# Layer 0 of a two-layer encoder: narrow weight chunks out, 512-column moving operands in, convolution run over two blocks at a time

## The chip, the cores and the metric

The kernel runs on one core of one Trainium2 chip. The metric is the device time of one execution in microseconds (us); the time before is the median of three runs. The engines are named as in the profile: PE (TensorE, the matrix unit), DVE (VectorE), ACT (ScalarE), POOL (GpSimd) and SP (SyncE, which issues the DMA transfers).

## What is computed

Two residual layers work on x, 256 positions by 2048 channels, all in fp32. Layer 0 is the one that the change touches; layer 1 (a gated linear recurrence in both directions) has the same outer form. Cut to layer 0, the reference is:

```python
h = rms_norm(x, conv_norm)                       # 256 x 2048
u = h @ w_in                                     # 2048 x 6144
a, b, z = jnp.split(u, 3, axis=-1)
v = a * jax.nn.sigmoid(b)
v = depthwise_conv(v, dw, taps=31, centred) + dw_b
v = jax.nn.silu(layer_norm(v, ln_g, ln_b))       # over the 2048 channels
x = x + (v * jax.nn.silu(z)) @ w_out             # 2048 x 2048
```

The layer norm runs over all channels at one position, so nothing behind it can start before the convolution of the last channel is there.

## The kernel before

**Products in high and low parts.** TensorE takes its operands in a rounded format (fp32r). So every fp32 weight piece (1 MB, `raw`, three buffers, loaded by SP) is cast by ACT to a high part `wh` (L133) and the remainder `wl` = raw - wh is taken (L134), by POOL for the in-projection of layer 0 (pieces 1 to 47; pieces 0 and 2 on DVE) and by DVE from piece 48 on. There are three buffers of each, so the cast of a piece waits until PE has done with the piece three before, and the load of a piece waits until the subtraction three before is done. The activations stand likewise as `hx`, high part and low part side by side. A product is wh·hi + wh·lo + wl·hi.

**The in-projection of layer 0.** The 2048 channels are taken in eight chunks j of 256. For each come a product `pa` (a) and a product `pb` (b), two weight pieces each (8 k-blocks of 128 input channels by 256 columns); after all eight, the eight products `pz` (the gate z). For j >= 2 a product is one `ws_chunk` (L207, which runs `ws_half`, L157 to L159, twice): 96 matmuls of 256 columns, all into one PSUM bank that holds both halves of the chunk. For j = 0 and 1 the work goes in half chunks of 128 channels (`ws_narrow`, L203 to L205). Layer 1 has another form, `pair_chunk` (L171 and L178): its moving operand is 512 columns, the high part and the low part of `hx` together, so a piece takes 16 matmuls of 512 columns with wh and 16 of 256 with wl. The result then has its wh·lo part in the other half of the bank, a chunk takes two banks, and a copy (ACT, L823) and an addition (DVE, L824) fold it. PSUM has four banks for all these products (tag "mm"), used in turn; a product begins when the bank that it takes has been read by its last reader.

**The convolution.** When pb of a chunk is done, ACT takes the sigmoid and DVE multiplies (`glu`). Then the 31 taps: ACT makes the first (`conv_start`, L411) and four more as products that POOL adds up (L423, L425); DVE makes the other 26 as fused multiply-adds with the accumulator in PSUM (L436) and the final sum `y` (L445). The two 128-channel blocks of a chunk are taken in turn, tap by tap, from j = 2 on; those of j = 0 and 1 each alone, behind their narrow chunk. POOL adds the finished blocks into a sum for the mean (L454, L456).

**Layer norm and gate.** After the last block PE forms the mean (`mu_ps`, L464), DVE subtracts it (L478), ACT squares, PE forms the variance (`var_ps`, L490), and then DVE goes chunk by chunk through scaling (L501), gain and offset (L508), products with the gate (L513, L514) and the low part (L516). Among these stand the gates of z: a sigmoid on ACT (L567) and a product on DVE (L570), which is the last reader of the bank of that `pz`. The out-projection of layer 0 (`po`, L195 to L197) needs all of it; behind it comes layer 1, whose first product is `psq`.

**What sets the order.** Each engine works through its own instructions in the order in which the program writes them. The program writes the matmuls piece by piece and, between them, work of the other engines, as given by a small estimate of their times: `later(LAG, glu)` puts a step off by LAG us of estimated time, the convolution is a generator that is charged TAP us for each tap, and the weight casts of piece i + 2 are written as piece i is begun. The constants are in a few lines at the top; what they set is only where in an engine's order a step stands.

## Time and profile before

| | us |
|---|---|
| median of three runs | 1007.8 |
| the three runs | 1007.01, 1007.8, 1008.5 |
| the profiled execution | 1008.56 |
| its span, first to last instruction | 1006.5 |
| PE busy in the span | 984.4 (98%) |
| DVE busy | 763.6 (76%) |
| ACT busy | 529.3 (53%) |
| POOL busy, all of it before 301 us | 254.0 (25%) |

The profiled execution took 1008.56 us in all, 2.1 us more than its span, and lies 0.76 us above the median. Layer 0 fills the first 401.8 us: the normalization and the first transposes to about 14 us, the a and b products to 212 us, the z products to 307.7 us, the out-projection to 401.8 us. What follows is layer 1, which the change leaves as it is.

### The profile page before, as it was taken

Reading aid. Unit: us, or ns where it says so; the run is one execution under the profiler, and the core shown is the slowest. Engines: PE = TensorE matmul, PEld = TensorE weight load, DVE = VectorE, ACT = ScalarE, POOL = GpSimd, SP = SyncE. Lnnn points to the kernel's source line nnn. Section 1 sums busy time; section 2 is a strip of 40 time slices with the busy share of each in tenths; the row PEclk is TensorE's granted clock in tenths of the full one; section 3 lists DMA queues with packets and bytes.
Section 4 is the critical chain, followed back from the end, with each engine's and each line's share of the span. In section 5 each row is a group of like instructions: output and inputs, shape, how many; then the busy total and the mean of one; then the engine's idle time right before and its main releaser. Section 6 shows DMA issues by size and latency. Waiting matters only on the chain.

```text
span 1006.5 us, 16189 instructions
## 1 busy us (share of the span) xinstructions
PE 984.4 (98%) x6657; PEld 876.4 (87%) x6657; DVE 763.6 (76%) x1228; ACT 529.3 (53%) x601; POOL 254.0 (25%) x107
## 2 busy tenths in 40 slices
PE   4999999999999999999999999999999999999998
PEld 4999999999997888888888888888888888888886
DVE  4587989888699455676878968889688897888552
ACT  6664655553656444555464644647456465465431
POOL 2499999999760000000000000000000000000000
PEclk9999999999999999999999999999999999999999
DMA  7765655555636655656545455554554536445561
GB/s 221 185 199 168 192 184 174 186 187 170 206 129 207 194 183 172 204 168 194 174 140 188 142 170 168 165 169 143 192 167 161 174 127 210 133 161 168 173 204 42
DMA packets 143995, 173.45 MB, mean 172 GB/s; under 512 B 2946, under 2 KB 109715, under 8 KB 143763
## 3 DMA queue, kind: packets, MB, share of 16 engines
q1 hardware_dynamic: 143922, 172.42, 53.1%
q8 instruction: 52, 0.85, 0.4%
q14 instruction: 21, 0.17, 0.1%
HBM read 170.31 MB, written 2.10 MB: 171 GB/s over the span
## 4 chain that ended last, share of the span: by engine, by line
PE 85%; POOL 5%; DVE 4%; DMA 3%; issue 2%; ACT 1%; SPq 0%; POOLq 0%; DVEq 0%; ACTq 0%
PE psaf L171 6%; PE psq L171 6%; PE psab L171 6%; PE lv L699 3%; POOL wl L134 3%; PE psaf L178 3%; PE psq L178 3%; PE psab L178 3%; PE po L196 3%; PE psz L195 3%; PE po L197 3%; PE pq L195 3%; PE po L195 3%; PE pq L196 3%; PE psz L197 3%; PE psv L195 3%
## 5 line engine op out<-in xcount | busy, mean ns | idle before, releaser
L133 ACT CAST wh<-raw 128x2048 fp32r<-128x2048 f32 (+1 forms) x172 | 306.6, 1788 | 296.8 <-issue 42.3
L134 DVE TENSOR_TENSOR wl<-raw,wh 128x2048 fp32r<-128x2048 f32 (+1 forms) x120 | 261.6, 2183 | 133.5 <-ACT wh L133 129.5
L134 POOL TENSOR_TENSOR wl<-raw,wh 128x2048 fp32r<-128x2048 f32 (+1 forms) x52 | 213.1, 4117 | 45.2 <-ACT wh L133 45.0
L436 DVE SCALAR_TENSOR_TENSOR acc<-vb,dw,acc 128x256 f32<-128x256 f32 x416 | 168.1, 482 | 7.5 <-ACT acc L411 6.4
L676 ACT COPY x<-T 128x512 f32<-128x512 f32 x88 | 55.9, 670 | 52.3 <-DVE T L684 51.9
L159 PE MATMUL pz<-hx,wl 128*128 128x256 f32 x256 | 72.6, 284 | 0.9 <-POOL wl L134 0.9
L157 PE MATMUL pz<-hx,wh 128*128 128x256 f32 x256 | 73.0, 285 | 0.0
L158 PE MATMUL pz<-hx,wh 128*128 128x256 f32 x256 | 72.4, 283 | 0.0
L171 PE MATMUL psaf<-hx,wh 128*128 128x512 f32 x256 | 63.5, 395 | 0.0
L171 PE MATMUL psab<-hx,wh 128*128 128x512 f32 x256 | 63.3, 394 | 0.0
L684 DVE TENSOR_TENSOR T<-T,pb 128x512 f32<-128x512 f32 x96 | 61.8, 685 | 1.3 <-PE lv L699 1.0
L171 PE MATMUL psq<-hx,wh 128*128 128x512 f32 x256 | 62.3, 392 | 0.0
L171 PEld LDWEIGHTS psq<-hx,wh 128*128 128x128 f32 x256 | 47.2, 188 | 9.6 <-DVE hx L247 0.3
L159 PE MATMUL pa<-hx,wl 128*128 128x256 f32 x192 | 54.7, 285 | 0.7 <-POOL wl L134 0.7
L159 PE MATMUL pb<-hx,wl 128*128 128x256 f32 x192 | 54.4, 284 | 0.2 <-POOL wl L134 0.2
L171 PEld LDWEIGHTS psaf<-hx,wh 128*128 128x128 f32 x256 | 46.4, 188 | 9.4
L158 PE MATMUL pb<-hx,wh 128*128 128x256 f32 x192 | 54.3, 283 | 0.0
L158 PE MATMUL pa<-hx,wh 128*128 128x256 f32 x192 | 54.3, 283 | 0.0
L157 PE MATMUL pb<-hx,wh 128*128 128x256 f32 x192 | 54.3, 283 | 0.0
L157 PE MATMUL pa<-hx,wh 128*128 128x256 f32 x192 | 54.3, 283 | 0.0
L171 PEld LDWEIGHTS psab<-hx,wh 128*128 128x128 f32 x256 | 46.4, 188 | 9.0
L707 DVE COPY_PREDICATED sd<-mask,lv 64x256 f32<-64x256 uint8 (+1 forms) x104 | 48.9, 470 | 7.0 <-PE lv L699 4.3
(201 smaller groups left out, 2320.1 us busy)
## 6 DMA issues: line engine op xcount, KB each, us to landing
raw<-in_hgrn_w_in SPq DMA_DIRECT2D x80, 1024.0 KB, 5.2
raw<-in_conv_w_in SPq DMA_DIRECT2D x47, 1024.0 KB, 5.3
raw<-in_conv_w_out SPq DMA_DIRECT2D x16, 1024.0 KB, 5.1
raw<-in_hgrn_w_out SPq DMA_DIRECT2D x16, 1024.0 KB, 5.1
out<-ot SPq DMA_DIRECT2D x8, 256.0 KB, 3.2
xt<-in_x SPq DMA_DIRECT2D x1, 1024.0 KB, 4.9
xt<-in_x SPq DMA_DIRECT2D x2, 512.0 KB
raw<-in_conv_w_in SPq DMA_DIRECT2D x4, 256.0 KB, 7.5
```

The source lines that it names most:

```text
L133: A.copy(wh[:, sl, :], raw[:, sl, :])
L134: eng.tensor_tensor(out=wl[:, sl, :], in0=raw[:, sl, :], in1=wh[:, sl, :].bitcast(F32), op=ALU.subtract)
L157: mm(ps[:, j, :], lhsT=a, rhs=hi[:, k, :], start=(k == 0 and j == 0), stop=False)
L158: mm(ps[:, j, :], lhsT=a, rhs=lo[:, k, :], start=False, stop=False)
L159: mm(ps[:, j, :], lhsT=wl[:, kk, j * P:(j + 1) * P], rhs=hi[:, k, :], start=False, stop=(k == KB - 1 and j == 1))
L171: mm(ps[j].rearrange("p a s -> p (a s)"), lhsT=wh[:, kk, j * P:(j + 1) * P], rhs=hx[:, k].rearrange("p a s -> p (a s)"), start=(k == 0), s ...
L178: mm(ps[j][:, 0, :], lhsT=wl[:, kk, j * P:(j + 1) * P], rhs=hx[:, k, 0, :], start=False, stop=(k == KB - 1))
L195: mm(ps[t], lhsT=a, rhs=wh[:, kk, :], start=(k == 0), stop=False)
L196: mm(ps[t], lhsT=a, rhs=wl[:, kk, :], start=False, stop=False)
L197: mm(ps[t], lhsT=lo[:, k, t * P:(t + 1) * P], rhs=wh[:, kk, :], start=False, stop=(k == KB - 1))
L436: ins = V.scalar_tensor_tensor(out=accs[j, u], in0=vb[:, u, c:c + S], scalar=dw[:, k, c:c + 1], in1=accs[j, u], op0=ALU.mult, op1=ALU.add)
L684: V.tensor_tensor(out=tv, in0=tv, in1=pv, op=ALU.mult)
```

## The change

Five things in layer 0 change. **Form:** all products but the first, pa of j = 0, become `pair_chunk`; there are no narrow chunks. Each then takes two PSUM banks of the four, and a new `fold` adds the low part: two copies on ACT into one SBUF tile `an0`, which has a single buffer, and 2.0 estimated us later two additions on DVE. **glu** works by halves, with the sigmoid in place in PSUM. **The gate** of z works by halves as well. **The convolution** is one generator over all chunks that runs two blocks as two lanes, the second begun when the first has 10 of its steps done; the four products are always made for both blocks together. **The first pieces**: pieces 0 to 3 are no longer 16 k-blocks of 128 columns but 8 of 256, still cast and split in four parts each (two k-blocks at a time), and the low part of piece 2 goes from DVE to POOL. The constants LAG (1.5 to 4.0) and TAP (.425 to .4) change.

```diff
-        eng = G if 1 <= i < n_a and i != 2 else V
-        step = nk if i > 3 else 4
+        eng = G if 1 <= i < n_a else V
+        step = nk if i > 3 else 2
...
-    def ws_narrow(ps, hi, lo):
...
+    def block_gen(j, u):
+        k = 2 * j + u
+        conv_start(j, u)
         for c in range(1, CW - NSIDE):
+            if u == 0 and c % SGAP == 2 and c // SGAP < NSIDE:
+                product(j, CW - NSIDE + c // SGAP)
+            chain(V.scalar_tensor_tensor(out=accs[j, u], in0=vbuf[j % NV][:, u, c:c + S], scalar=dw[:, k, c:c + 1],
+                                         in1=accs[j, u], op0=ALU.mult, op1=ALU.add))
+            yield
+        chain(V.tensor_tensor(out=y[:, k, :], in0=accs.pop((j, u)), in1=sides[j][:, u, :], op=ALU.add))
+        add_y(k)
...
+    def conv_gen():
+        while lanes or ready:
+            if ready and (not lanes or len(lanes) == 1 and lanes[0][1] >= OFFSET):
+                lanes.append([block_gen(*ready.pop(0)), 0])
+            if ready and len(lanes) == 2 and lanes[0][1] >= INIT:
+                conv_start(*ready[0])
+            for lane in list(lanes):
+                lane[1] += 1
+                if next(lane[0], 0) == 0:
+                    lanes.remove(lane)
                 yield TAP
...
+    def fold(ps, to=None):
+        for h in range(2):
+            A.copy(an0[:, h, :], ps[h][:, 1, :])
+
+        def add():
+            for h in range(2):
+                V.tensor_tensor(out=ps[h][:, 0, :] if to is None else to[:, h, :], in0=ps[h][:, 0, :],
+                                in1=an0[:, h, :], op=ALU.add)
+
+        later(FOLD, add)
...
-        pa = pmm.tile([P, 2, S], F32, tag="mm", name=f"pa{j}")
-        run(ws_chunk(pa, hh, hl), TK)
-        pb = pmm.tile([P, 2, S], F32, tag="mm", name=f"pb{j}")
-        run(ws_chunk(pb, hh, hl), TK)
-        A.activation(sg, pb, AF.Sigmoid)
+        else:
+            pa = [pmm.tile([P, 2, S], F32, tag="mm", name=f"pa{j}_{h}") for h in range(2)]
+            run(pair_chunk(pa, hx), TK)
+            fold(pa, at)
+        pb = [pmm.tile([P, 2, S], F32, tag="mm", name=f"pb{j}_{h}") for h in range(2)]
+        run(pair_chunk(pb, hx), TK)
+        fold(pb)
...
+            for h in range(2):
+                A.activation(pb[h][:, 0, :], pb[h][:, 0, :], AF.Sigmoid)
+                V.tensor_tensor(out=vb[:, h, :], in0=at[:, h, :], in1=pb[h][:, 0, :], op=ALU.mult)
...
-        pz = pmm.tile([P, 2, S], F32, tag="mm", name=f"pz{j}")
-        run(ws_chunk(pz, hh, hl), TK)
-        sg = ca.tile([P, 2, S], F32, tag="sg", name=f"sgz{j}", bufs=3)
-        A.activation(sg, pz, AF.Sigmoid)
+        pz = [pmm.tile([P, 2, S], F32, tag="mm", name=f"pz{j}_{h}") for h in range(2)]
+        run(pair_chunk(pz, hx), TK)
+        fold(pz)
...
+            sg = ca.tile([P, 2, S], F32, tag="sg", name=f"sgz{j}", bufs=3)
+            for h in range(2):
+                A.activation(sg[:, h, :], pz[h][:, 0, :], AF.Sigmoid)
+                V.tensor_tensor(out=sz[:, 2 * j + h, :], in0=pz[h][:, 0, :], in1=sg[:, h, :], op=ALU.mult)
```

In the changed kernel the lines have other numbers: casts L128 and low parts L129, taps L421, `conv_start` L397, products L409, fold copies L513 and fold additions L517, the sigmoid of glu L547, the gate product of z L565; in the layer norm the scaling is L490, gain and offset L497, the products with the gate L502 and L503, the low part L505. Three places show how rows stand.

ACT at the start, from the casts of piece 2 to the first tap of the convolution (`acc0_0`), before and then after. `an0` is the fold's tile; the table loads belong to an exponential and to the sigmoid.

```order
L133 CAST wh2_192<-raw2_166 128x512 x4
L133 CAST wh3_313<-raw3_178 128x512 x4
L537 ACT_TABLE_LOAD
L537 ACTIVATE sg0_164<-pb0_0_312 128x256
L369 ACT_TABLE_LOAD
L369 ACTIVATE lbw_397<-lbw_397 128x64
L133 CAST wh4_410<-raw4_190 128x2048
L411 ACTIVATE acc0_0_432<-vb0_142,pvec_115,dw_117 128x256
```

```order
L128 CAST wh4_375<-raw4_190 128x2048
L128 CAST wh5_413<-raw5_202 128x2048
L128 CAST wh6_490<-raw6_295 128x2048
L513 COPY an0_152<-pb0_0_373 128x256
L513 COPY an0_152<-pb0_1_374 128x256
L356 ACT_TABLE_LOAD
L356 ACTIVATE lbw_476<-lbw_476 128x64
L547 ACT_TABLE_LOAD
L547 ACTIVATE pb0_0_373<-pb0_0_373 128x256
L547 ACTIVATE pb0_1_374<-pb0_1_374 128x256
L128 CAST wh7_548<-raw7_379 128x2048
L397 ACTIVATE acc0_0_530<-vb0_142,pvec_115,dw_117 128x256
```

The casts of pieces 5 and 6 now stand ahead of the first tap, and the first tap follows both halves of pb.

ACT in the middle of the convolution, around the end of pb of chunk 4, before and then after.

```order
L133 CAST wh20_1538<-raw20_1327 128x2048
L133 CAST wh21_1607<-raw21_1399 128x2048
L133 CAST wh22_1683<-raw22_1473 128x2048
L553 ACTIVATE sg4_1393<-pb4_1537 128x512
L411 ACTIVATE acc4_0_1741<-vb1_145,pvec_115,dw_117 128x256
```

```order
L513 COPY an0_152<-pb4_0_1284 128x256
L513 COPY an0_152<-pb4_1_1285 128x256
L128 CAST wh23_1466<-raw23_1290 128x2048
L547 ACTIVATE pb4_0_1284<-pb4_0_1284 128x256
L128 CAST wh24_1522<-raw24_1349 128x2048
L513 COPY an0_152<-pa5_0_1405 128x256
L547 ACTIVATE pb4_1_1285<-pb4_1_1285 128x256
L513 COPY an0_152<-pa5_1_1406 128x256
L397 ACTIVATE acc4_0_1457<-vb1_145,pvec_115,dw_117 128x256
```

The sigmoid of pb's second half has moved behind the cast of piece 24 and behind the copy out of `pa5_0`, which is the product that PE makes next.

DVE in the layer norm, around the gate of z's chunk 5 (`sz` from `pz5`), before and then after; `wl48` is the low part of the out-projection's first weight piece.

```order
L508 TENSOR_SCALAR y_73<-y_73,pvec_115 128x256 x2
L513 TENSOR_TENSOR lsg4_3386<-sz_74,lsg4_3386 128x512
L516 TENSOR_TENSOR yl0_3244<-lsg3_3358,yh0_3243 128x512
L514 TENSOR_TENSOR lsg4_3386<-y_73,lsg4_3386 128x512
L501 TENSOR_TENSOR y_73<-y_73,var_ps_3220 128x512
L570 TENSOR_TENSOR sz_74<-pz5_3253,sgz5_3407 128x512
L501 TENSOR_TENSOR y_73<-y_73,var_ps_3220 128x512
```

```order
L502 TENSOR_TENSOR lsg4_2849<-sz_74,lsg4_2849 128x512
L517 TENSOR_TENSOR pz5_0_2700<-pz5_0_2700,an0_152 128x256
L503 TENSOR_TENSOR lsg4_2849<-y_73,lsg4_2849 128x512
L517 TENSOR_TENSOR pz5_1_2701<-pz5_1_2701,an0_152 128x256
L490 TENSOR_TENSOR y_73<-y_73,var_ps_2712 128x512
L505 TENSOR_TENSOR yl0_2728<-lsg4_2849,yh0_2727 128x512
L565 TENSOR_TENSOR sz_74<-pz5_0_2700,sgz5_2888 128x256
L497 TENSOR_SCALAR y_73<-y_73,pvec_115 128x256 x2
L565 TENSOR_TENSOR sz_74<-pz5_1_2701,sgz5_2888 128x256
L490 TENSOR_TENSOR y_73<-y_73,var_ps_2712 128x512
L502 TENSOR_TENSOR lsg5_2877<-sz_74,lsg5_2877 128x512
L129 TENSOR_TENSOR wl48_2950<-raw48_2778,wh48_2949 128x2048
```

The gate of chunk 5 stands at the same place in the layer norm as before, behind the products of the fifth chunk, now with its fold ahead of it and in two halves.

## Rows read from the trace of the kernel before

**Rows 1.** The page's first part: busy time and share of each engine.

```profile
PE 984.4 (98%) x6657; PEld 876.4 (87%) x6657; DVE 763.6 (76%) x1228; ACT 529.3 (53%) x601; POOL 254.0 (25%) x107
```

**Rows 2.** Stretches: length, busy PE, PEld, DVE, ACT, POOL; granted clock, DMA share, GB/s.

```profile
30.00:60.00 30.00, 28.92 (x237) 28.76 (x236) 20.80 (x53) 20.87 (x28) 21.67 (x11) 0.94 0.77 209
90.00:120.00 30.00, 30.00 (x251) 30.00 (x252) 23.44 (x57) 14.95 (x17) 29.92 (x11) 1.00 0.59 182
300.00:330.00 30.00, 27.64 (x147) 23.81 (x146) 25.62 (x31) 17.36 (x18) 0.88 (x1) 0.94 0.60 198
```

**Rows 3.** Timeline of PE: start, us, line, instructions; out-projection's start, layer 1's first product.

```profile
307.70 0.50 PE L195 MATMUL po<-wh,yh 128*128 128x512 f32 x1
310.56 0.80 PE L196 MATMUL po<-wl,yh 128*128 128x512 f32 x1 [2.36 <-DVE wl L134]
...
401.80 1.08 PE L171 MATMUL psq<-hx,wh 128*128 128x512 f32 x4
```

**Rows 4.** Stretches again: one ws chunk (pa) and one pair chunk (psab), start to start.

```profile
71.93:83.45 11.52, 11.52 (x99) 11.52 (x97) 10.75 (x29) 6.41 (x8) 11.44 (x6) 1.00 0.58 183
425.59:436.73 11.14, 11.14 (x67) 9.85 (x65) 7.71 (x10) 6.75 (x8) 0.00 (x0) 1.00 0.56 191
```

**Rows 5.** Timeline of PE: the first piece of that pair chunk.

```profile
425.59 3.82 PE L171 MATMUL psab<-hx,wh 128*128 128x512 f32 x16
429.25 2.08 PE L178 MATMUL psab<-hx,wl 128*128 128x256 f32 x16
```

**Rows 6.** Timeline of ACT near the start, with idle time before and its releaser.

```profile
32.24 2.18 ACT L133 CAST wh<-raw 128x512 fp32r<-128x512 f32 x4 [4.29 <-DMA raw<-in_conv_w_in]
...
38.11 1.28 ACT L537 ACT_TABLE_LOAD   x1
39.40 0.38 ACT L537 ACTIVATE sg<-pb 128x256 f32<-128x256 f32 x1
```

**Rows 7.** POOL's groups: line, operation, shapes, count, busy us, mean ns, idle before.

```profile
L134 POOL TENSOR_TENSOR wl<-raw,wh 128x2048 fp32r<-128x2048 f32 x44 | 203.1, 4632 | 15.2 <-ACT wh L133 15.0 <-PE mu_ps L464 0.2
L425 POOL TENSOR_TENSOR prods<-prods 128x512 f32<-128x512 f32 x18 | 23.4, 1298 | 0.4
L134 POOL TENSOR_TENSOR wl<-raw,wh 128x512 fp32r<-128x512 f32 x8 | 10.0, 1282 | 30.0 <-ACT wh L133 30.0
```

**Rows 8.** Timeline of PE: the vectors' transposes, the fifth product, the first of z.

```profile
33.32 0.23 PE L353 MATMUL tp_v<-ident,stage 80*128 80x80 f32 x1
...
48.89 0.28 PE L203 MATMUL pa<-hx,wh 128*128 128x256 f32 x1
...
211.99 0.28 PE L157 MATMUL pz<-hx,wh 128*128 128x256 f32 x1
```

**Rows 9.** Timeline of DVE: the first taps, and taps of two blocks in turn.

```profile
43.72 8.43 DVE L436 SCALAR_TENSOR_TENSOR acc<-vb,dw,acc 128x256 f32<-128x256 f32 x16 [0.67 <-ACT acc L411]
...
100.21 18.99 DVE L436 SCALAR_TENSOR_TENSOR acc<-vb,dw,acc 128x256 f32<-128x256 f32 x48 [0.64 <-ACT acc L411]
```

**Rows 10.** Layer 1's fold addition: ns, least, median and most; first and last start.

```profile
L824 DVE TENSOR_TENSOR anaf<-psaf,anaf x16: 412/416/425, 428.1 to 871.3; 128x256 f32<-128x256 f32 x16
```

**Rows 11.** The page's sixth part: loads of the in-projection's pieces, KB each, us to landing.

```profile
raw<-in_conv_w_in SPq DMA_DIRECT2D x47, 1024.0 KB, 5.3
```

**Rows 12.** Timeline of ACT: a weight cast in the convolution.

```profile
118.62 1.91 ACT L133 CAST wh<-raw 128x2048 fp32r<-128x2048 f32 x1 [3.85 <-PE pb L158]
```

**Rows 13.** Timelines of PE, DVE and POOL: from the mean to the gate of z5.

```profile
254.53 1.02 PE L464 MATMUL mu_ps<-y,ones 128*128 128x256 f32 x4
...
293.58 7.45 DVE L508 TENSOR_SCALAR y<-y,pvec 128x256 f32<-128x256 f32 x2
...
303.34 0.68 DVE L570 TENSOR_TENSOR sz<-pz,sgz 128x512 f32<-128x512 f32 x1
...
291.62 9.26 POOL L134 TENSOR_TENSOR wl<-raw,wh 128x2048 fp32r<-128x2048 f32 x2 [6.30 <-ACT wh L133]
```

**Rows 14.** Gain and offset of the layer norm: groups of one line, and its least/median/most ns.

```profile
L508 DVE TENSOR_SCALAR y<-y,pvec 128x256 f32<-128x256 f32 x16 | 19.3, 1218 | 1.6 <-ACT lsg L505 1.6
L508 DVE TENSOR_SCALAR y<-y,pvec x16: 396/402/4700, 276.9 to 312.5; 128x256 f32<-128x256 f32 x16
```

More of the change, by code (lines that the diff above doesn't have):

```diff
@@ L69, in add @@
             plan.append((w, k0, nk, c0, ncol))
-    for u in range(2 * NARROW):
-        add(w_cin, u * P, P)
-        add(w_cin, D + u * P, P)
-    for j in range(NARROW, NCH):
+    for j in range(NCH):
         add(w_cin, j * CH, CH)
@@ L402, in trunk @@
     count = [0]
[L403 to L404 removed]
+    prods = big.tile([P, KB // 2, 2, S], F32, tag="yh", name="prods")
     def conv_start(j, u):
@@ new lines, in trunk, with product @@
+    sides = {}
+    def product(j, c):
+        if j in sides:
+            pr = prods[:, 2 + count[0] % 3]
+            count[0] += 1
+        else:
+            pr = prods[:, j % 2]
+        for u in range(2):
+            A.activation(pr[:, u, :], vbuf[j % NV][:, u, c:c + S], AF.Copy, scale=dw[:, 2 * j + u, c:c + 1])
+        if j in sides:
+            G.tensor_tensor(out=sides[j], in0=sides[j], in1=pr, op=ALU.add)
+        else:
+            sides[j] = pr
+    def block_gen(j, u):
+        k = 2 * j + u
+        conv_start(j, u)
+        for c in range(1, CW - NSIDE):
+            if u == 0 and c % SGAP == 2 and c // SGAP < NSIDE:
[5 more added lines that the diff above has]
+        add_y(k)
@@ L549, in trunk @@
-        pa = pmm.tile([P, 2, S], F32, tag="mm", name=f"pa{j}")
-        run(ws_chunk(pa, hh, hl), TK)
-        pb = pmm.tile([P, 2, S], F32, tag="mm", name=f"pb{j}")
-        run(ws_chunk(pb, hh, hl), TK)
-        A.activation(sg, pb, AF.Sigmoid)
-        def glu(j=j, pa=pa, sg=sg, vb=vb):
-            V.tensor_tensor(out=vb, in0=pa, in1=sg, op=ALU.mult)
-            ready.append((j, 0))
-            bg.append(conv_gen(j, (0, 1)))
+        at = prods[:, 5 + j % 2]
+        if j == 0:
+            pa = pmm.tile([P, 2, S], F32, tag="mm", name=f"pa{j}")
+            for _ in ws_chunk(pa, hh, hl):
+                next(h0, None)
+            A.copy(at, pa)
+        else:
+            pa = [pmm.tile([P, 2, S], F32, tag="mm", name=f"pa{j}_{h}") for h in range(2)]
+            run(pair_chunk(pa, hx), TK)
+            fold(pa, at)
@@ new lines, in trunk, with glu @@
+        pb = [pmm.tile([P, 2, S], F32, tag="mm", name=f"pb{j}_{h}") for h in range(2)]
+        run(pair_chunk(pb, hx), TK)
+        fold(pb)
+        if j == 0:
+            for _ in vec_gen():
+                pass
+        def glu(j=j, at=at, pb=pb, vb=vb):
+            for h in range(2):
+                A.activation(pb[h][:, 0, :], pb[h][:, 0, :], AF.Sigmoid)
+                V.tensor_tensor(out=vb[:, h, :], in0=at[:, h, :], in1=pb[h][:, 0, :], op=ALU.mult)
+            ready.extend(((j, 0), (j, 1)))
+            if not bg:
+                bg.append(conv_gen())
```

76 lines of the change are left out of this document (7 added, 69 removed).

## The prediction, made before the changed kernel had run

> **What bounds the kernel now.** I read the page's busy times first, then a table of stretches, then the timelines of PE, ACT, DVE and POOL around the places that the change touches. PE is busy 98% of the span [rows 1], and in a stretch of the convolution it is busy all 30.00 us of 30 [rows 2]. So the matrix work sets the end, and two things can move it: less PE time for each product, or new waits on PE. POOL is as close: in the same 30 us it is busy 29.92, and DVE 23.44 [rows 2]. The granted clock is 1.00 there; it is 0.94 at 30 to 60 us and at 300 to 330 us [rows 2], in each of which PE had stood still: for the transposes of the vectors, and for 2.36 us on a low part at the start of the out-projection [rows 3]. 0.06 of 30 us is 1.8 us of full clock; in round numbers such a wait costs 1.7 us more than its own length.
>
> **The form of the product.** A ws chunk takes 11.52 us, a pair chunk of layer 1 takes 11.14 [rows 4], 5.57 a half. Of a half the 16 matmuls of 512 columns take 3.66 us, from their start to that of the next row [rows 5], and the 16 of 256 the remaining 1.91. The saving is 0.38 us a chunk, and 23 of 24 chunks change: 8.8 us of PE. This is the whole direct gain. It is measured in the same kernel with the same shapes, so I take it as certain wherever PE has its operands.
>
> The row of the 512-column matmuls gives 3.66/16 = 229 ns each, and the ws chunk gives 11.52/96 = 120 ns for 256 columns: the 512-column one costs 11 ns less than two of the others [rows 4, 5]. The Trainium skill, "TensorE: Matmul & The Clock Gate", section "Wait — 56ns, not 53.3ns?", has a fixed cost of about 2.5 ns for each matmul above the columns at 2.4 GHz; by it 32 matmuls fewer in a chunk would save 0.08 us, 1.8 us over 23 chunks in place of 8.8. The rows are of this kernel, so they decide; by the page the forecast below would be some 7 us higher.
>
> **Start.** The first product keeps its form. Piece 2 comes late from memory: ACT waits 4.29 us for it and casts from 32.24 [rows 6]; the change leaves when it is asked for as it is. Low parts 2 and 3 are now both on POOL, in four parts of 1.28 us each [rows 7]: piece 2 from about 32.8 to 37.9, piece 3 to 43.0. pb of chunk 0 ends 0.2 to 1.9 us later, 43.2 to 44.9. Before, the vector transposes began at 33.32; back from the fifth product at 48.89 [rows 8], 1.7 us of clock and two narrow products of 5.76 (half of 11.52) lead to 35.7, so the transposes with their wait took 2.4 us, and still do. With the 1.7 us of clock the fifth piece starts at 47.3 to 49.0; I take 48.9, no gain, since nothing hides POOL here.
>
> **Convolution, PE side.** From the fifth piece on 28 halves of 5.57 us stand ahead of z: 48.9 + 155.9 = 204.8 us, against 211.99 [rows 8]. That is 7.2 us earlier, if nothing waits.
>
> Two resources must keep up. **POOL** had for two products four low parts of 4.63, three sums of 1.30 [rows 7] and two block sums at half of that, an estimated 0.7 each: 23.8 us, and it was busy 29.92 of 30 [rows 2]. The six chunks from 71.93 [rows 4] to 211.99 [rows 8] took 23.34 each against 23.04 of matmuls, so POOL already sets the pace a little, and now PE asks for two products in 22.3. POOL's part is unchanged, so add it up: from 43.0, 29 low parts (pieces 4 to 32) of 4.63 and some 6.6 chunks of sums at 5.3 give 134.3 + 35.0, so 212.3 for piece 32, the first of z; PE wants that 3.66 us into the product. So z starts at about 208.7 even if nothing else waits, not at 204.8; of the 7.2 us some 3.3 are left. In z itself POOL has two low parts, 9.3 us, in 11.1 and is ahead.
>
> DVE has for a pair 52 taps at 18.99/48 = 0.394 to the next start (0.396) [rows 9], and two last sums, two products of glu and four fold additions, each like a fold addition of layer 1 at 0.42 or a little under to the next start, say 0.33 [rows 10]: 20.6 + 2.6 = 23.2 us. Its first taps come later. In ACT's order the casts of pieces 4 to 6 now stand ahead of pb's fold; piece 6 can be asked for when the low part of piece 3 is done, about 43, and a load takes 5.3 us [rows 11], so its cast ends near 50; two copies, two table loads of 1.28 [rows 6], the sigmoids and the first tap make the first DVE tap about 56 to 57, against 43.72 [rows 9]. From 57, eight pairs of 23.2 and some 5 us for folds and gates of z give the last y at about 248. Unlike the first taps, that is in time for the mean (below).
>
> **Waits for a bank.** This is the new cost. A pair chunk takes two of the four banks, so pb of chunk j + 1 needs the banks of pb of chunk j, one chunk of 11.1 us after that ended. They come free with glu. From chunk 4 on, ACT's order has the second sigmoid of glu behind the cast of the piece three uses on, and a cast waits for PE to finish the piece whose buffer it takes (3.85 us of waiting, then 1.91 us, in [rows 12]). That cast can start only when the product between has ended, which is the very moment at which PE wants the bank; in chunk 4 the sigmoid is behind a copy out of that product as well. So PE waits for a cast or copy (0.37 to 1.9 us partly overlapped), a sigmoid (0.38 [rows 6]) and a multiplication (0.42): 0.7 to 1.4 us, at pb of chunks 5 to 7 and z of chunk 0 to 4. Before, no row shows such a wait, because a chunk takes one bank of four. The bounds are 0 (POOL or DVE delay nothing and the sigmoids run in the cracks) and 1.4 each; Those before z take time in which POOL is behind anyway, and they go on POOL's account: z starts at 208.7 to 210, I take 209. For the four of z that lie before the mean I take 0.85 each, 3.4 us.
>
> **From the mean to the out-projection.** The last part of the mean stands in PE's order in the middle of z's chunk 4 (before, of chunk 3). With 4.5 chunks of 11.14 = 50.1 us, that is reached at 209 + 3.4 + 50.1 = 262.5, and the mean is done at 263.0 (call it t; 260 without any bank wait, 266 with all at 1.4 and a later start of z). The last y is there at 248, so it doesn't wait. Before, the mean's last matmuls began at 254.53 and ended about 255.2, and the gate of z5 ended at 304.0 [rows 13]: 48.8 us later. Nothing waited for that gate, because PE had banks to spare. Now z's chunk 7 needs both banks of chunk 5, and in DVE's order the gate of z5 still stands behind the layer norm of the fifth chunk. On PE only 2.5 chunks, the variance and a short wait lie between t and that point: 27.9 + 1.7 = t + 29.6.
>
> How long does DVE take? In the 48.8 us there are holds: the gain-and-offset operation takes 0.40 us at the median and up to 4.70 [rows 14]; two took 7.45 while POOL ran low parts for 9.26 [rows 13]. All 16 took 19.3 us [rows 14], 12.9 more than 16 x 0.40. Without them the way is 35.9; halved gates and folds add about 1.2, so t + 37 without holds. POOL has one chunk's low parts fewer left than before, so I count one hold of some 6 us: t + 43. Bounds: t + 37 and t + 50. So z's chunk 7 waits 13 us (7 to 20), with 1.7 for the clock; then come its 11.1 us. The out-projection took 401.80 - 307.70 = 94.1 us, of which 2.4 was a wait for the low part and 1.7 clock [rows 2, 3]; both go, because DVE makes that low part while PE is on chunk 7: 90.0 us. Layer 1's first product then starts at t + 43 + 11.1 + 1.7 + 90.0 = 408.8, against 401.80 [rows 3]: **7.0 us later**. From there the work is the same. The span becomes 1013.5, the profiled execution 1015.6, and the median 1007.8 + 7.0 = **1014.8**.
>
> **Rivals.** (A) *The banks come free in time*: glu and the gates run ahead of PE's need, no bank wait binds, and only POOL and the PE time count. z starts at 208.7 and ends 8 x 11.14 + 1.6 later at 299.4, and the out-projection takes 90.0 to 94.1: 389.4 to 393.5, a gain of 8 to 12 us, 996 to 1000. For it: the gate of z5 is a matter of order, and DVE is only 78% busy [rows 2]. Against it: the excerpt of DVE's order and the 48.8 us. Chance 0.24. (B) *No waits before the mean, and hardly a hold*: t is 260, the gate at t + 37 to 41, z's chunk 7 waits 7 to 11 us: 399.8 to 403.8, from 2 us earlier to 2 us later, 1005.8 to 1009.8; the saving of the form and the new wait cancel. Chance 0.22, a third of it on the faster side if the gate needs a little less still. (C) *Each short wait takes the clock along*: the eight short waits cost PE time of their own beside POOL's, and half of them are followed by 1.7 us of lost clock: 7 to 12 us on the forecast, 1021 to 1027. For it: both stretches with a clock of 0.94 follow a wait of PE [rows 2, 3, 8]. The Trainium skill, in "TensorE: Matmul & The Clock Gate", section "A second HAM failure mode: psum-queue depth-cycling", tells of the same: short idle times between groups as banks are cycled, and the clock goes down and up. No run shows it here for waits of a microsecond. Chance 0.12.
>
> **How the numbers follow.** The end is t + g + 102.8, where t is 260 to 266 and g is 37 to 50, so every microsecond of either moves the result by one; where the banks don't bind it is (A). The forecast case (t near 263, g 41 to 47, 1010 to 1019) has 0.42. A measurement of this kernel can tell about 0.2%, 2 us, from no change. Faster is A and a third of B: 0.32. Same is the rest of B: 0.14. Slower is the forecast and C: 0.54. The range leaves out the foot of A and most of C: 996 to 1021.
>
> **What would show it.** Right: z's chunk 7 starts more than 7 us after chunk 6 ends, and the releaser is the gate of z5 on DVE; short waits on PE at pb from chunk 5, released by glu; a pair chunk of 11.1 us between; first taps near 57 us; z from about 209. Wrong: PE without a wait in z (A); gain-and-offset operations of 0.40 us throughout (B); a granted clock under 0.97 between 100 and 250 us (C); a mean that waits for the last y, which would mean that DVE or POOL, not the banks, sets the pace.

## The result and the profile after

The changed kernel takes **1021.04 us** (median of four runs, 1020.65 to 1021.75) against 1007.85 for the kernel before, run beside it: 1.0127 times as long, 95% interval 1.0114 to 1.0140, 13.2 us slower. The forecast was 1014.8, slower by 7.0, with a range to 1021. The direction was right, the size a little over half of what came, and the median lies 0.04 us above the end of the range.

The page's first part of the kernel after, as [rows 1]:

```profile
PE 978.4 (96%) x5921; PEld 837.0 (82%) x5921; DVE 778.0 (76%) x1284; ACT 541.5 (53%) x661; POOL 257.6 (25%) x105
```

PE has 6.0 us less work in a span that is 13.4 us longer: 19 us more of PE standing still. The stretches of the kernel after, columns as in [rows 2] and [rows 4]:

```profile
94.69:105.83 11.14, 11.14 (x67) 9.85 (x66) 11.14 (x30) 5.70 (x10) 11.14 (x5) 1.00 0.44 142
150.00:180.00 30.00, 25.75 (x135) 21.89 (x133) 22.73 (x60) 15.67 (x23) 29.84 (x12) 0.89 0.59 188
300.00:330.00 30.00, 19.43 (x92) 15.99 (x91) 27.78 (x48) 17.19 (x29) 0.63 (x1) 0.77 0.34 111
```

The first is one product in its new form: 11.14 us, exactly what layer 1's pair chunk took [rows 4]. PE, DVE and POOL are all busy for the whole of it. The other two are where the time went: PE stood still, and the granted clock fell while it did (0.89 and 0.77 as means over 30 us; 1.2 GHz, half of the full 2.4, for 6.8 us from 153.1 and for 13.7 us from 303.3).

The five largest groups of waits of PE in layer 0 (PE's line, what it waited for; us in total, times, longest), kernel after:

```profile
PE pz L166 <- DVE sz L565: 12.3, 3, 10.5
PE pb L166 <- DVE vb L548: 6.0, 4, 4.3
PE pb L166 <- ACT wh L128: 2.5, 1, 2.5
PE pa L166 <- DVE prods L517: 2.2, 1, 2.2
PE mu_ps L453 <- POOL bcb L445: 1.5, 1, 1.5
```

The first, second and fourth are waits for a bank: the releasers are the gate of z, the multiplication of glu and the fold. The kernel before had none of them. On PE's timeline (as [rows 3] and [rows 8]):

```profile
46.42 0.50 PE L166 MATMUL pa<-hx,wh 128*128 128x512 f32 x1
...
155.01 1.22 PE L166 MATMUL pb<-hx,wh 128*128 128x512 f32 x2 [4.25 <-DVE vb L548]
...
214.69 0.40 PE L166 MATMUL pz<-hx,wh 128*128 128x512 f32 x1
...
271.30 0.59 PE L453 MATMUL mu_ps<-y,ones 128*128 128x256 f32 x2
...
311.30 1.19 PE L166 MATMUL pz<-hx,wh 128*128 128x512 f32 x2 [10.54 <-DVE sz L565]
...
325.35 0.40 PE L190 MATMUL po<-wh,yh 128*128 128x512 f32 x1
...
415.29 1.08 PE L166 MATMUL psq<-hx,wh 128*128 128x512 f32 x4
```

Layer 1 starts at 415.29 against 401.80 [rows 3]: 13.5 us later, the whole loss. What follows takes as long as before.

| | before | forecast | after |
|---|---|---|---|
| fifth piece (pa of chunk 1) | 48.89 | 48.9 | 46.42 |
| first tap on DVE | 43.72 | 56 to 57 | 60.60 |
| first product of z | 211.99 | 209 | 214.69 |
| last y | 253.1 | 248 | 270.3 |
| mean done (t) | 255.2 | 263.0 | 271.5 |
| z's chunk 7 begins | | t + 43 | 311.30, t + 39.8 |
| out-projection, start to layer 1 | 94.1 | 90.0 | 89.9 |
| layer 1 starts | 401.80 | 408.8 | 415.29 |

### The profile page after: what moved, and what is told of

It reads as the page before. It is cut to its first block, busy times and chain, and to the rows that moved or that the text cites. A ratio compares the mean times of both kernels' runs of the same rounds, so it can differ in the third digit from the quotient of the medians.

```text
span 1019.9 us, 14847 instructions
## 1 busy us (share of the span) xinstructions
PE 978.4 (96%) x5921; PEld 837.0 (82%) x5921; DVE 778.0 (76%) x1284; ACT 541.5 (53%) x661; POOL 257.6 (25%) x105
## 4 chain that ended last, share of the span: by engine, by line
PE 72%; DVE 2%; POOL 1%; ACT 1%; issue 1%; DVEq 0%; ACTq 0%
PE psaf L166 6%; PE psq L166 6%; PE psab L166 6%; PE pz L166 4%; PE lv L694 3%; PE psaf L173 3%; PE psq L173 3%; PE psab L173 3%; PE pq L190 3%; PE psz L190 3%; PE pq L191 3%; PE po L190 3%; PE psv L190 3%; PE psz L191 3%; PE psv L192 3%; PE po L192 3%
## 5 line engine op out<-in xcount | busy, mean ns | idle before, releaser
L128 ACT CAST wh<-raw 128x2048 fp32r<-128x2048 f32 (+1 forms) x172 | 306.7, 1789 | 298.5 <-issue 52.0
L129 DVE TENSOR_TENSOR wl<-raw,wh 128x2048 fp32r<-128x2048 f32 (+1 forms) x116 | 259.3, 2236 | 133.5 <-ACT wh L128 129.4
L129 POOL TENSOR_TENSOR wl<-raw,wh 128x2048 fp32r<-128x2048 f32 (+1 forms) x56 | 217.9, 3920 | 41.5 <-ACT wh L128 41.5
L421 DVE SCALAR_TENSOR_TENSOR acc<-vb,dw,acc 128x256 f32<-128x256 f32 x416 | 170.9, 483 | 2.8 <-ACT acc L397 1.8
L166 PE MATMUL pz<-hx,wh 128*128 128x512 f32 x256 | 65.5, 407 | 13.5 <-DVE sz L565 12.3
L166 PE MATMUL pb<-hx,wh 128*128 128x512 f32 x256 | 65.2, 404 | 8.6 <-DVE vb L548 6.0
L166 PEld LDWEIGHTS pz<-hx,wh 128*128 128x128 f32 x256 | 48.6, 195 | 25.2 <-ACT lsg L494 10.7
L166 PEld LDWEIGHTS pb<-hx,wh 128*128 128x128 f32 x256 | 48.5, 195 | 19.6 <-DVE vb L548 7.3
L166 PE MATMUL pa<-hx,wh 128*128 128x512 f32 x224 | 53.9, 393 | 2.2 <-DVE prods L517 2.2
L702 DVE COPY_PREDICATED sd<-mask,lv 64x256 f32<-64x256 uint8 (+1 forms) x104 | 48.9, 470 | 7.0 <-PE lv L694 4.3
L190 PE MATMUL psz<-wh,hx 128*128 128x512 f32 x128 | 50.6, 395 | 0.0
L190 PE MATMUL po<-wh,yh 128*128 128x512 f32 x128 | 50.4, 394 | 0.0
L190 PE MATMUL psv<-wh,hx 128*128 128x512 f32 x128 | 50.4, 394 | 0.0
L190 PE MATMUL pq<-wh,yh 128*128 128x512 f32 x128 | 50.3, 393 | 0.0
```

The source lines that it names most:

```text
L128: A.copy(wh[:, sl, :], raw[:, sl, :])
L129: eng.tensor_tensor(out=wl[:, sl, :], in0=raw[:, sl, :], in1=wh[:, sl, :].bitcast(F32), op=ALU.subtract)
L166: mm(ps[j].rearrange("p a s -> p (a s)"), lhsT=wh[:, kk, j * P:(j + 1) * P], rhs=hx[:, k].rearrange("p a s -> p (a s)"), start=(k == 0), s ...
L190: mm(ps[t], lhsT=a, rhs=wh[:, kk, :], start=(k == 0), stop=False)
L421: chain(V.scalar_tensor_tensor(out=accs[j, u], in0=vbuf[j % NV][:, u, c:c + S], scalar=dw[:, k, c:c + 1], in1=accs[j, u], op0=ALU.mult, op ...
L702: V.copy_predicated(sd[es, :, es], mask[es, li:li + 1, es].broadcast_to([hw, 4, hw]), lv[es, :, es])
```

## The experiments

Each kernel is the change with the edit shown (e8, e10, e11 and e12 have several). "Off the change" means how far its median lies under 1021.04; ratios are to the kernel before, run beside it. That kernel took 1007.85 us beside the change and 1008.02 to 1008.51 beside the experiments, so a difference of under a microsecond says nothing.

**e1: z in one bank.** The products of z and their gate go back to the old form.

```diff
-        pz = [pmm.tile([P, 2, S], F32, tag="mm", name=f"pz{j}_{h}") for h in range(2)]
-        run(pair_chunk(pz, hx), TK)
-        fold(pz)
+        pz = pmm.tile([P, 2, S], F32, tag="mm", name=f"pz{j}")
+        run(ws_chunk(pz, hh, hl), TK)
...
```

> z alone goes back to the old form: one bank, 96 matmuls of 256 columns, gate in one piece; a and b keep the new form. Theory B (banks: a product that takes two of four banks waits for the gate of the product two before): z's chunk 7 no longer waits 10.7 us, the half clock behind it is gone, z products take 11.5 us each; z starts at 214.7 as now, the mean waits some 4 us for the last y at 270, z ends near 312.5, layer 1 starts near 406.5 instead of 415.3: about 1012 us. Rival L (the layer norm's chain from the mean sets the start of the out-projection, and the bank wait only shows it): the wait moves to the first matmuls of the out-projection, 8 us or more, and the time stays at 1019 to 1021 us.

1011.46 us, ratio 1.0033 (1.0021 to 1.0045): 9.6 off the change, as theory B had it, although z's matmuls are 3 us longer. Waits of PE from 200 to 330 us in e1:

```profile
PE po L191 <- DVE wl L129: 4.1, 1, 4.1
PE pb L166 <- DVE vb L548: 0.8, 1, 0.8
```

No wait in z is left. The old wait for the low part of the out-projection's first piece is back [rows 3], so rival L gets a little of it. The edit takes away z's folds together with its second bank, but the gate tells the two apart: that of z's chunk 5 is as late after the mean as before the edit (written at 309.4, some 40 us after the mean was done at 269.0; 312.4 and 271.5 in the change), and PE has made all of chunk 7 by then, 308.0. So it is the bank that held PE there. The gate's row on DVE in e1:

```profile
308.76 0.68 DVE L563 TENSOR_TENSOR sz<-pz,sgz 128x512 f32<-128x512 f32 x1
```

**e7: one bank everywhere.** All products in the old form, without narrow chunks and with the new convolution: e1's edit for z, and the same for a and b.

```diff
-        pb = [pmm.tile([P, 2, S], F32, tag="mm", name=f"pb{j}_{h}") for h in range(2)]
-        run(pair_chunk(pb, hx), TK)
-        fold(pb)
+        pb = pmm.tile([P, 2, S], F32, tag="mm", name=f"pb{j}")
+        run(ws_chunk(pb, hh, hl), TK)
+        A.activation(sg, pb, AF.Sigmoid)
...
```

> The new form is taken back everywhere: all 24 products have one bank and 96 matmuls of 256 columns, no folds, glu and gate in one piece; no narrow chunks, the convolution in two lanes as in the change. It tells what the rest of the change is worth without the form. Theory B: no wait for a bank at all, 8.8 us more of matmuls than with the change, z starts at 211 to 213 (POOL's pace), the last y at 250 to 255, 1004 to 1009 us: the form with its folds and banks is the whole loss. Rival (the lanes and the later first tap cost as much): last y at 260 or later, 1012 us or more.

1008.86 us, ratio 1.0010 (1.0000 to 1.0019). So the new form, with its folds and its two banks, is the whole loss; beside the old form, the rest of the change is worth nothing that could be told from zero. z starts at 211.7, as theory B had it. The last y comes at 258.2, between the two theories, and still ahead of the mean's place in PE's order (264.4), so it cost only slack.

**e2: the gate of chunk 5 earlier.** The layer norm's second chunk waits, in the program, until that gate is written.

```diff
-            while j not in zdone:
+            while j not in zdone or j == 1 and 5 not in zdone:
```

> The new form everywhere; only the gate of z's chunk 5 is written ahead of the second chunk of the layer norm instead of behind the fifth. Theory B: the gate is done near 298 instead of 312, z's chunk 7 follows chunk 6 at 300.6 without a wait, 10.7 us and 2.7 us of half clock are saved: layer 1 starts near 402, about 1008 us. Rival L: the out-projection waits for the layer norm instead, less than half is saved, 1014 us or more.

1020.04 us, ratio 1.0119 (1.0102 to 1.0136): 1.0 off the change, which its interval doesn't tell from no gain. z's chunk 7 waits 1.4 us instead of 10.5, but the out-projection, which takes the same four banks, now waits for the gate of chunk 6 (3.7 us) and, at 333.6 us, for that of chunk 7 (0.6). Waits of PE from 290 to 330 us in e2:

```profile
PE po L190 <- DVE sz L565: 3.7, 1, 3.7
PE pz L166 <- DVE sz L565: 1.4, 1, 1.4
```

Rival L was right on the size. It is still the banks that hold PE, but of whichever gate stands behind the layer norm; to move one of them hands the wait on.

**e9: gain and offset on ACT.**

```diff
-                V.tensor_scalar(out=d[:, u, :], in0=d[:, u, :], scalar1=lng[:, k:k + 1], scalar2=lnb[:, k:k + 1],
-                                op0=ALU.mult, op1=ALU.add)
+                A.activation(d[:, u, :], d[:, u, :], AF.Identity, bias=lnb[:, k:k + 1], scale=lng[:, k:k + 1])
```

> The change, with only the layer norm's gain and offset (16 operations on DVE) made on ACT. With the change three of them took 3.04 us and one 3.52, to the ends of two low parts on POOL, 5.0 us above their usual time, all ahead of the gate of z's chunk 5. Theory H (holds by POOL lengthen the way from the mean to that gate): the gate is done 6 to 8 us sooner after the mean, the wait of z's chunk 7 falls from 10.7 to 3 to 5 us, about 1014 us. Rival (ACT becomes the bound of the chain with 8 us more work): the gate stays within 2 us, 1020 us or more.

1016.93 us, ratio 1.0083 (1.0068 to 1.0098): 4.1 off the change; it would be 7 by the expectation. In its profile, the longest of its four executions (1020.91, the others 1015.14 to 1017.36), the gate is done 35 us after the mean instead of 41 and z's chunk 7 waits 5.9 us instead of 10.5. The holds are real; in the kernel after they look like this (DVE, then POOL):

```profile
292.18 3.04 DVE L497 TENSOR_SCALAR y<-y,pvec 128x256 f32<-128x256 f32 x3 [1.13 <-ACT lsg L494]
...
297.26 3.52 DVE L497 TENSOR_SCALAR y<-y,pvec 128x256 f32<-128x256 f32 x1
...
289.80 4.63 POOL L129 TENSOR_TENSOR wl<-raw,wh 128x2048 fp32r<-128x2048 f32 x1 [1.93 <-ACT wh L128]
296.02 4.61 POOL L129 TENSOR_TENSOR wl<-raw,wh 128x2048 fp32r<-128x2048 f32 x1 [1.60 <-ACT wh L128]
```

The operation at 297.26 ends at 300.78, when POOL's low part ends at 300.63; of the three at 292.18 the first takes 2.39 us, to 294.57, when the low part before that had ended at 294.43. The Trainium skill, "SBUF — State Buffer", section "Who interferes with whom", says that DVE in some modes, a tensor-scalar operation among them, and GpSimd use one pair of ports, and that the later one is blocked. The trace agrees, with 3.52 us where 0.40 is usual.

**e3 and e5: sigmoids first.** glu writes its two sigmoids one behind the other. The framework that lays out the instructions put the second behind a cast and a copy, as the order of ACT shows. An ordering edge without a semaphore puts casts and fold copies behind the last sigmoid; in e5 the sigmoids of the gate of z too.

```diff
+    def behind(ins):
+        if sigs:
+            tc.add_manual_dep(ins.ins, sigs[-1], ...)
...
-            A.copy(wh[:, sl, :], raw[:, sl, :])
+            ins = A.copy(wh[:, sl, :], raw[:, sl, :])
+            if step == nk:
+                behind(ins)
...
-            A.copy(an0[:, h, :], ps[h][:, 1, :])
+            behind(A.copy(an0[:, h, :], ps[h][:, 1, :]))
...
-                A.activation(pb[h][:, 0, :], pb[h][:, 0, :], AF.Sigmoid)
+                sigs.append(A.activation(pb[h][:, 0, :], pb[h][:, 0, :], AF.Sigmoid).ins.name)
```

> On ACT both sigmoids of glu stand ahead of the next weight cast and the next fold copy; nothing else is changed. Theory O (order: the second sigmoid behind a cast that waits for its load holds the bank): pb of chunk 5 waits under 1 us instead of 4.65, its half clock goes, z starts near 208.5, the last y near 265, about 1015 us. Rival P (POOL's pace: low parts come too late for the shorter products anyway): the waits go over to low parts, released by POOL, and z starts at 212 or later, 1018 us or more.

> As the kernel with glu's sigmoids first, and the sigmoids of the gate of z stand ahead of the next cast and fold copy as well. There z started at 209.6 instead of 214.7, but DVE then stood 7.0 us at the gate of z's chunk 0, and the last y came at 271.4, no earlier than with the change. Theory D (the last y, hence the mean and all behind it, is set by DVE, which stands still wherever one of its instructions is behind a cast on ACT): that wait goes, the last y comes near 264.5, the gate of chunk 5 near 305, about 1015 us. Rival B alone (only banks on PE count): PE was not held by DVE there, so nothing is gained over 1022 us.

e3: 1022.36 us, ratio 1.0144 (1.0126 to 1.0161), no gain. Yet in its profile no product of a or b waits for glu, and z starts at 209.6 instead of 214.7: theory O is right about that place. All of it is lost again in z: DVE waits there for the sigmoids of the gate, which ACT holds behind casts, PE waits 5.7 us for a bank which that gate holds, with 6.8 us of half clock from 234.6, and the last y comes at 271.4. So PE was held by DVE there, other than the expectation of e5 has it. DVE's waits from 200 to 272 us in e3, and PE's row:

```profile
DVE sz L575 <- ACT sgz L574: 12.8, 3, 7.0
...
238.11 0.77 PE L176 MATMUL pz<-hx,wh 128*128 128x512 f32 x1 [5.71 <-DVE sz L575]
```

e5 takes that away as well: 1017.07 us, ratio 1.0098 (1.0077 to 1.0120), 4.0 off the change, with executions from 1016.12 to 1020.73; z starts at 207.5, the last y comes at 267.5. Theory D expected 264.5 and 1015. DVE no longer waits for a sigmoid of the gate, but for a copy of z's fold, which now stands behind the sigmoids (200 to 272 us in e5):

```profile
DVE pz L527 <- ACT an L523: 8.3, 1, 8.3
```

**e4: POOL without its sums.** The three sums of products of each chunk are left out, so three of the 31 taps are missing from the output.

```diff
-        if j in sides:
-            G.tensor_tensor(out=sides[j], in0=sides[j], in1=pr, op=ALU.add)
-        else:
+        if j not in sides:
             sides[j] = pr
```

> The three sums of products on POOL are left out of every chunk of the convolution (only the first product is added in the end), so POOL has 3.9 us less for two products; ACT and DVE do what they did. Theory P: loads and casts are no longer late, no wait of pb above 1 us, z starts near 206 to 208; the wait of z's chunk 7 stays at 8 to 12 us; about 1013 us. Theory O alone: the cast still stands ahead of the sigmoid and still waits for PE's buffer, so pb of chunk 5 still waits over 1 us, z starts at 211 or later, 1017 us or more.

1015.04 us, ratio 1.0085 (1.0058 to 1.0111): 6.0 off the change, the middle between the two theories. In its profile PE waits 0.9 us at pb of chunk 5 instead of 4.25, though the cast still stands ahead of the sigmoid. Waits of PE from 100 to 210 us in e4:

```profile
PE pb L166 <- DVE vb L546: 1.7, 2, 0.9
```

But this profile can't be put down to the edit alone. It is the longest of its five executions (1021.48, the others 1014.52 to 1018.44), and it has the long hold at the start that is described under e6: pa of chunk 1 waits 8.8 us there, PE comes later to all that follows, and z begins at 216.2. The profile of e9 has the same hold and all of POOL's sums, and the wait at pb of chunk 5 is 1.14 us there; in that of e6, which keeps the sums too, it is 1.72 (PE in e9, then in e6):

```profile
158.90 0.50 PE L166 MATMUL pb<-hx,wh 128*128 128x512 f32 x1 [1.14 <-DVE vb L547]
...
150.84 0.50 PE L166 MATMUL pb<-hx,wh 128*128 128x512 f32 x1 [1.72 <-DVE vb L553]
```

So the order on ACT is shown to be a cause of that wait by e3. POOL's lateness is shown by who releases the load in the change itself (below), and e4's median fits it; that e4's edit removes the wait is not shown.

**e6: the forget bounds late.** Ten small operations for layer 1 stand at the start, behind the transposes of the vectors. With the change POOL runs low parts at that time (DVE, then POOL, kernel after):

```profile
45.81 0.99 DVE L353 TENSOR_TENSOR lbw<-pvec 128x32 f32<-128x32 f32 x1
46.73 0.66 DVE L347 COPY dw<-tp_dw 128x496 f32<-128x496 f32 x1
47.31 4.09 DVE L354 TENSOR_TENSOR lbw<-pvec,lbw 128x32 f32<-128x32 f32 x1
51.33 4.64 DVE L355 TENSOR_TENSOR lbw<-pvec,lbw 128x32 f32<-128x32 f32 x1
...
60.60 11.22 DVE L421 SCALAR_TENSOR_TENSOR acc<-vb,dw,acc 128x256 f32<-128x256 f32 x25 [1.82 <-ACT acc L397]
...
32.14 23.79 POOL L129 TENSOR_TENSOR wl<-raw,wh 128x512 fp32r<-128x512 f32 x11 [8.31 <-ACT wh L128]
```

Operations of 32 columns took 4.09 and 4.64 us; their like two lines on took 0.17. The edit moves them behind the out-projection, with an ordering edge:

```diff
-            for _ in vec_gen():
-                pass
+            vg = vec_gen()
+            next(vg)
...
```

> Only the small operations on layer 1's forget bounds (ten on DVE with 32 columns, one exponential with its table load on ACT) move from the start to the out-projection. With the change three of the DVE ones took 0.99, 4.09 and 4.64 us, each to the end of a low part on POOL, and the first tap came at 60.6. Theory D: first tap at 51 to 53, last y some 4 to 8 us earlier, the waits of pa of chunk 2 (2.45) and pb of chunk 1 (0.86) go, about 1016 us. Rival (the conv catches up anyway, POOL and the banks set the pace): the last y stays at 268 or later, 1020 to 1021 us.

1018.15 us, ratio 1.0102 (1.0087 to 1.0117): 2.9 off the change. First tap at 53.4, last y at 266.6, mean done 3.7 us earlier: theory D, at a little over half of its size. Its profile has z start at 209.2, 5.5 us earlier than the change, with 1.72 us of waiting at pb of chunk 5 and no half clock near it; part of that is lost in z, where chunk 1 waits 2.3 us, with 3.4 us of half clock from 224.3. In the profiles of e4 and e9 the first of these operations was held for 9.97 and 9.95 us, and pa of chunk 1 waited 8.8 us for the copy behind it. The executions of e4 lie up to 7.0 us apart and those of e9 5.8; those of e6 lie within 0.34.

**e8, e10 and e11: the cures together.** a and b in the new form, z in one bank (e1), glu's sigmoids first (e3), bounds late (e6), and the low part of the out-projection's first piece on POOL. e10 changes in addition the estimated time of a tap, which moves the mean in PE's order from behind 469 of z's 768 matmuls to behind 412; e11 is e10 with gain and offset on ACT.

```diff
-        eng = G if 1 <= i < n_a else V
+        eng = G if 1 <= i < n_a + 1 else V
...
-TAP, WAIT, WEND, WS, LAG, FOLD = .4, 9.5, 7.0, 2.0, 4.0, 2.0
+TAP, WAIT, WEND, WS, LAG, FOLD = .385, 9.5, 7.0, 2.0, 4.0, 2.0
```

> The new form for a and b, one bank for z, glu's sigmoids first, the forget bounds late, and the low part of the out-projection's first piece on POOL instead of DVE. Theory (banks in z, order on ACT, holds at the start, each seen alone): z starts near 207, the last y near 250, z ends near 301, the out-projection starts without a wait, layer 1 near 392, about 998 us. Rival L (the layer norm's chain then sets the start of the out-projection): waits of 4 to 8 us at its first matmuls, 1002 to 1006 us.

> As the kernel with all cures; only the estimated time of a tap goes from .400 to .385, which puts the last part of the mean in PE's order at 412 of the 768 matmuls of z instead of 469. There DVE stood 11.2 us for the mean with the last y done at 254.6, and the out-projection then stood 5.5 us for the gate of z's chunk 5. Theory: the mean is done near 257.5 instead of 265.4, that gate near 301.5, the out-projection's wait and its half clock go, layer 1 starts near 394, about 1000 us. Rival (POOL's low parts hold PE in z, the last y moves back): the mean at 262 or later, 1005 us or more.

> The same with gain and offset on ACT as well. Theory: the layer norm's chain has some 10 us of slack then, nothing waits at the out-projection, 391 to 393 for layer 1, 998 to 1000 us, little better than without. Rival: ACT, with 8 us more ahead of casts, holds z's last products: 1002 us or more.

e8: 1007.57 us, ratio 0.9994 (0.9985 to 1.0004), level with before; both numbers expected were missed. z starts at 203.9, 8 us earlier than before, and the last y is there at 254.6. But the mean stands too late in PE's order, and DVE waits for it; what is late next is the gate of chunk 5 and the out-projection. DVE's wait from 240 to 272 us and PE's longest from 290 to 330 us in e8:

```profile
DVE y L482 <- PE mu_ps L468: 11.2, 1, 11.2
```

```profile
PE po L200 <- DVE sz L578: 5.1, 1, 5.1
```

e10: **1004.58 us**, ratio 0.9966 (0.9954 to 0.9979), 3.4 us better than before: both kernels are beaten. 1000 was expected; the mean is done at 261.4 instead of 257.5, because PE waits for low parts and glu on the way, and both numbers lie nearer to the rival's (262, 1005). Waits of PE in layer 0 in e10:

```profile
PE pz L164 <- POOL wl L139: 4.7, 4, 1.6
PE pb L176 <- DVE vb L563: 3.6, 3, 1.9
PE pb L176 <- ACT wh L136: 2.0, 1, 2.0
PE po L201 <- DVE wl L139: 0.7, 1, 0.7
```

No wait is over 2.0 us, and in its profile the granted clock stays up throughout layer 0. Where z, the out-projection and layer 1 begin in it:

```profile
206.95 0.28 PE L162 MATMUL pz<-hx,wh 128*128 128x256 f32 x1
...
307.04 0.40 PE L200 MATMUL po<-wh,yh 128*128 128x512 f32 x1
...
397.90 0.61 PE L176 MATMUL psq<-hx,wh 128*128 128x512 f32 x2
```

Against the kernel before (211.99, 307.70 and 401.80 [rows 3, 8]) its profiled execution gains 5.0 us up to z, loses 4.4 in z and gains 3.2 in the out-projection, whose old wait for a low part and the half clock behind it [rows 2, 3] are gone with the low part on POOL. That last gain comes from a cure, not from the form. No run has the old form with these cures, so how much of the 3.4 us the form brings is not shown.

e11: 1005.88, ratio 0.9981 (0.9972 to 0.9990), not better than e10, as its rival said; but the rival named ACT, and in the profile POOL's low parts hold PE, for 6.3 us in z.

**e12: two banks for z as well, with the cures** (sigmoids first in glu and gate, bounds late, gain and offset on ACT).

> The new form everywhere, z too, with the other cures: sigmoids of glu and gate first, forget bounds late, gain and offset on ACT. Each alone took 4.0, 2.9 and 4.1 us off the change. Theory B (a product of z in two banks must wait for the gate of the product two before, which stands behind the layer norm of the fifth chunk): z's chunk 7 still waits, 4 to 8 us, the mean is done near 263 and that gate near 298, about 1007 to 1010 us, more than the 1004.6 of the kernel with one bank for z. Rival (once the holds and the order are mended, two banks do for z as well): no wait over 2 us in z, 1002 us or less.

1005.79 us, ratio 0.9979 (0.9968 to 0.9990): better than before, and its interval overlaps that of e10. In z no wait is over 2.1 us, so theory B missed the place; the wait for a gate has gone over to the out-projection, which the rival missed. Waits of PE from 200 to 330 us in e12:

```profile
PE po L200 <- DVE sz L579: 4.0, 1, 4.0
PE pz L183 <- POOL wl L139: 2.1, 1, 2.1
```

## Why the prediction was right in direction and short in size

Layer 1 starts 6.5 us later than forecast. By the steps of the prediction: t is 8.5 us later (271.5 for 263.0), the way from the mean to z's chunk 7 is 3.2 shorter (39.8 for 43), that chunk takes 14.05 where 11.1 + 1.7 was counted (1.2 more), and the out-projection 0.1 less: 8.5 - 3.2 + 1.2 - 0.1 = 6.4, the rest rounding. Of the 8.5 us, 5.7 lie ahead of z. In z the waits ahead of the mean came to 3.65 us for the 3.4 counted, and the mean's last part stands behind 292 of z's 512 matmuls, a little past the middle of chunk 4.

**Right: the form.** 11.14 us a product, as the row of layer 1 said. By the fixed cost of 2.5 ns a matmul (the Trainium skill, "TensorE: Matmul & The Clock Gate", "Wait — 56ns, not 53.3ns?") the saving on 11.52 would, as an estimate, have been 0.08 a product; it is 0.38, and the measurement decides.

**Right: the wait at z's chunk 7.** Its place, its releaser (the gate of z5 behind the fifth chunk of the layer norm) and its size (10.5 for 13, in bounds of 7 to 20) are as forecast, and e1 shows it by undoing the form of z alone. The out-projection's 90.0 came as 89.9, with both of its old losses gone. The holds were counted at 6 and were 5.0 (3.04 - 1.20 and 3.52 - 0.40); without them the way from the mean is 34.8 for the 37 counted.

**Mis-sized: the price of a bank wait.** The step said 0.7 to 1.4 us each, with the cast waiting for PE. That at chunk 5 was 4.25 us, and the clock fell in it; that product took 17.95 us from start to next start, 6.8 more than 11.13. That is more than the 5.7 us by which z began late; the fifth piece had begun 2.5 us early. The kernel after at that place, POOL and the load first, then ACT and DVE:

```profile
142.04 4.63 POOL L129 TENSOR_TENSOR wl<-raw,wh 128x2048 fp32r<-128x2048 f32 x1
...
146.70 0.37 SPq L112 DMA_DIRECT2D raw<-in_conv_w_in  x1
...
145.30 1.92 ACT L128 CAST wh<-raw 128x2048 fp32r<-128x2048 f32 x1 [3.99 <-DMA raw<-in_conv_w_in]
147.12 0.37 ACT L547 ACTIVATE pb<-pb 128x256 f32<-128x256 f32 x1
152.05 1.90 ACT L128 CAST wh<-raw 128x2048 fp32r<-128x2048 f32 x1 [4.57 <-DMA raw<-in_conv_w_in]
153.86 0.37 ACT L513 COPY an<-pa 128x256 f32<-128x256 f32 x1
154.12 0.38 ACT L547 ACTIVATE pb<-pb 128x256 f32<-128x256 f32 x1
...
154.53 0.42 DVE L548 TENSOR_TENSOR vb<-prods,pb 128x256 f32<-128x256 f32 x1 [5.72 <-ACT pb L547]
```

The cast at 152.05 waits for its load, not for PE. The load waits for POOL: a buffer for raw weights comes free when POOL's subtraction three pieces back is done, here at 146.67, and the load is issued at 146.70. POOL, which the prediction had found 1.5 us short for two products, had fallen that far behind. The prediction had both halves, put POOL's on its own account and the order's on another, and did not see that they meet at this cast: a late low part makes a late load, the load a late cast, and behind the cast stands the sigmoid that frees PE's bank. e3 takes away the order, and the wait is gone. POOL's half was to go in e4, whose profile leaves open whether that did it. How late POOL is at this place also hangs on the start, for in e6 the wait was 1.72 us and z began at 209.2. So this term and the holds at the start (below) can't be added up.

**Wrong: the last y has time.** 248 was forecast, 270.3 came. DVE's own work was right: 190.9 us busy from 60 to 271 us, for 191 counted. Not counted were 19 us in which DVE stood still, by the kernel's waits 10.2 of them for the sigmoids of glu, 4.3 for those of the gate and 3.2 for the copies of the fold, and, beside these, the later first tap. An instruction of DVE that waits for ACT holds all taps behind it. In the change itself y was no later than PE (the mean's last matmuls at 271.30, 1.0 us behind it), so it cost little by itself: 1.5 us, for which PE waited at the mean's first matmul for POOL's sum of the blocks. In e3, where z began 5.1 us earlier, the last y at 271.4 would have kept the mean where it was even if PE had not waited for a bank.

**Missed: the holds at the start.** The prediction let the first tap come 13 us later for casts and table loads. It did not see that the ten small operations now fall into POOL's low parts. 2.9 us, by e6. On the other side the start of the fifth piece was 2.5 us earlier than forecast, and in this execution the clock did not fall there.

**The rivals.** (A) and (B) did not happen. (C) did in part: in the kernel after, half clock came with the waits of 4.25 and 10.5 us and with none of the others, 0.4 to 2.5 us; between 100 and 250 us the mean granted clock was 0.98, over the 0.97 that was to show (C). The wait of 2.2 us at pa of chunk 2, without half clock here, was followed by 3.4 us of it in e1 and e5, from 72 us on, and in e3 and e6 waits of 1.7 us at the start were, at 33.2. Of waits of about a microsecond that stood alone none was; that of 1.08 us in the kernel before, which comes right behind the transposes, was, at 37.0 us.

What stays open: by how much POOL's pace alone would hold the new form. e10 still has 4.7 us of waits for low parts in z, and no run took that away. Open too is what the new form is worth once the order is mended, for want of a run of the old form with the same cures.

## What to carry to other kernels

A faster form that takes twice the PSUM banks halves how far PE may run ahead of its readers; before counting the saving, follow the reader of each bank through the orders of all engines that it passes, and see what it stands behind. Where two of the causes meet in one queue (a late load, and an instruction that others need behind it), count the wait from the later of them, not each for itself. Undo the form at each of its places apart: here the new form of z's eight products cost 9.6 us net of 3.0 of saving. With the order mended, kernels with the new form came out 2.1 to 3.4 us ahead of the kernel before, but cures that the old form could have had are in that sum.
